# Hybrid attention block on one core: half of the second query column as three rounded products behind the first key half, and lambda's vectors in a buffer of their own

## The chip, the cores and the metric

The kernel runs on one core of a Trainium2 chip. The core has a matmul engine (TensorE, PE in the profile, with PEld for its weight loads), VectorE (DVE), ScalarE (ACT), GpSimd (POOL) and SyncE (SP), which only issues transfers. Each engine works through its own instructions in order; engines wait for each other through semaphores. The metric is the device time of one execution in microseconds (us).

## The reference

A decoder block over 16 meta tokens and 512 positions of width 1024. It normalises the rows, projects them to ten column groups, runs two attention branches, gates and merges them, projects once more and normalises again. What matters here is the first projection and the first attention unit (differential attention, 8 heads, two score maps per head):

```python
h = layer_norm(concat(meta, x), emb_ln_g, emb_ln_b)              # 528 x 1024
lam = exp(sum(lp[0] * lp[1])) - exp(sum(lp[2] * lp[3])) + lam_init
proj = einsum('bld,dn->bln', h, w_in)                            # q_d k_d v_d g_d q_s k_s v_s g_s m_d m_s
s = q k^T / 8 + alibi                                            # two maps per head
a = softmax(s[0]) - lam * softmax(s[1])
y_d = rms_norm(a v, diff_subln_g) * (1 - lam_init)
...
h = layer_norm(DN_ALPHA * h + y, ln_g, ln_b)
```

Everything is float32. Only rows of 512 positions leave the kernel; the meta tokens serve as keys and values.

## The kernel before

The block is laid out with channels on the 128 partitions and positions along the free dimension. hF holds the normalised and scaled input in 8 blocks of channels (k = 0 to 7), each 528 positions wide. A projection of 128 output columns is a sum over the 8 blocks.

**Two kinds of product.** Most products are made of three "rounded" ones: a float32 number a is split into a rounded high part (hTh for the input, wh for a weight) and the rest (hTl, wl), and wh·hTh + wh·hTl + wl·hTh is summed in PSUM. A weight half (4 blocks k) is split by `hi` (ACT makes wh) and `lo` (DVE makes wl) into one of six buffers called w2; four of the eight halves loaded first (raw0) are numbered 0 to 3 for the two query columns, 4 and 5 for the first keys, 6 and 7 for the first values. The two query columns of the first two heads are an exception: `query` multiplies plain float32 operands, one matmul for each k, so it needs no split of hF and can start as soon as a block of hF exists.

**The beginning** is written out by hand in `order`, a string of short steps which are issued in this order to all engines: `S`, `N` statistics and normalisation of a block of 128 positions; `tij` transposes (PE); `aik` scale and shift into hF (ACT; `d` the same on DVE); `xik` the first query column for block i and channel block k (128 positions wide); `yhk` the second query column for half h (256 positions wide); `shk` and `hhk` the high part hTh of half h on ACT and on DVE; `lhk` the low part hTl (DVE); `Hnc`, `Lnc` the weight splits of half 2n+c; `meta`, `hm`, `lm` the meta tokens' part; `lam0`, `lam1`, `lam2` the two sums, the exponentials and the final value of lambda.

**Then** come `q_hi` and `q_lo`, which split the query columns from PSUM (ACT and DVE), and `stage_k` for the first unit: `proj_pos` makes two halves of 264 positions, each 24 matmuls in its own PSUM bank; each finished half is copied out by a chain of six steps that alternate between ACT and DVE (L637 to L642). `stage_v` does the same for values (two more banks). The function `then`, called at time 2.7 of the little clock in `run`, splits the second query column. The scores (`logits`, L764) use two PSUM banks in turn, and each is released by the DVE step at L844, which adds the bias and takes the minimum. The tile scheduler then orders the instructions of each engine; `keep_order` fixes that order as far as the first value stage.

**Memory.** The pool `start` holds what only the beginning needs (inputs, rows, lambda's vectors, sums). It is closed before the pool `att` is opened, which lies in the same memory: the first writer of each `att` tile waits until the last reader of the `start` tiles under it is done. On POOL the first such writers are own_block (L595), the bias ramp (L826 to L829) and the zeros of the key tiles (L607).

Of the kernel before, what the change touches and what calls it, by code (L numbers as in the profile page):

```python
# [9 lines left out]
F32 = mybir.dt.float32  # L10
# [6 lines left out]
P = 128  # L17
D = 1024
KT = D // P
S = 512  # L20
M = 16
# [4 lines left out]
LAM_INIT = 0.8 - 0.6  # L26
# [20 lines left out]
def hybrid_block_kernel(ctx: ExitStack, tc: tile.TileContext, x, meta, emb_g, emb_b, w_in, b_gate,  # L47
                        diff_lambda, subln_g, w_br_d, w_br_s, w_out, ln_g, ln_b, out):
    nc = tc.nc
    v, s, g, pe = nc.vector, nc.scalar, nc.gpsimd, nc.tensor  # L50
# [6 lines left out]
    const = ctx.enter_context(tc.tile_pool(name="const", bufs=1))  # L57
# [3 lines left out]
    gpool = ctx.enter_context(tc.tile_pool(name="g", bufs=6))  # L61
# [3 lines left out]
    pj = ctx.enter_context(tc.tile_pool(name="pj", bufs=3, space=PSUM))  # L65
# [109 lines left out]

    def hi(h):

        assert len(split) == h
        item = items[h]
        assert not second.get(item)  # L180
        raw = raw0[:, h // 2, ts(h % 2, 4)] if item is None else sums.pop(h) if isinstance(item, tuple) else raws[item]
        w2 = wpool.tile([P, 2, 4, P], F32R, tag="w2", name="w2", bufs=6)
        wh, wl = w2[:, 0], w2[:, 1]
        split.append((raw, wh, wl))
        s.copy(wh, raw)  # L185

    def lo(h, eng=v):
# [64 lines left out]
    xts = [sp.tile([P, D], F32, name=f"xt{i}") for i in range(NB)]  # L252
    xns = [sp.tile([P, D], F32, name=f"xn{i}") for i in range(NB)]
    mt = sp.tile([P, D], F32, name="mt")[:M]
    small = sp.tile([P, 512], F32, name="small")
    rows2, lamb = small[:17, :P], small[:, P:P + 256].rearrange("p (a d) -> p a d", a=4)
    for i in range(2):
        for o in (ts(0, 512), ts(1, 512)):
            nc.sync.dma_start(xts[i][:, o], x[0, ts(i, P), o])
# [90 lines left out]
    def q_hi(n):  # L350
        s.activation(A0[n][0], pss[n], AF.Copy, scale=0.125)
        s.activation(A0[n][1][LO], pss[n][HI], AF.Copy, scale=0.125)

    def q_lo(n):
        for c, own, _ in reversed(HEADS):
            v.scalar_tensor_tensor(A0[n][c][HI], pss[n][own], 0.125, A0[n][0][own].bitcast(F32), op0=ALU.mult,
                                   op1=ALU.subtract)
# [79 lines left out]
        tps[1] += banks(SC, SC, TP)  # L437


    lsum = sp.tile([P, 2], F32, name="lsum")  # L440
    lscr = sp.tile([P, 64], F32, name="lscr")
    lexp = sp.tile([P, 2], F32, name="lexp")

    def lam0():
        for c in range(2):
# [6 lines left out]
    def lam2():  # L452
# [5 lines left out]
    steps["t"] = lambda i, j: turn(i, tps[i // 2], range(2 * j, 2 * j + 2))  # L458
    steps["F"] = fill
    steps["H"], steps["L"] = lambda n, c: hi(2 * n + c), lambda n, c: lo(2 * n + c)  # L460
    words = dict(lam0=lam0, lam1=lam1, lam2=lam2, hm=lambda: s.copy(hTh[:, :, :M], hM), lm=low_meta, norm0=norm0, mnorm=mnorm, mturn=mturn, meta=meta, more=more_banks,
                 m0=lambda: stats(4, 0), m1=lambda: stats(4, 1), mr=lambda: rstd(4))

    def order(text):
        for step in text.split():
            if step in words:
                words[step]()
            else:
                steps[step[0]](*map(int, step[1:]))

    order("""S0 norm0 t00 t01 t02 t03 S1 F2 a00 a01 a02 a03 a04 a05 d06 d07 x00 x01 x02 x03 x04 x05 N1 t10 t11 x06 x07 t12 t13
             a10 a11 a12 a13 a14 a15 a16 a17 S2 m0 m1 mr N2 S3 mnorm
             x10 y00 x11 y01 x12 y02 x13 y03 t20 more t21 t22 t23 x14 y04 x15 y05 x16 y06 x17 y07
             a20 a21 a22 a23 a24 a25 a26 a27 H20 H21 x20 x21 x22 x23 N3 t30 t31 t32 t33 x24 x25 x26 x27 mturn
             a30 a31 a32 a33 a34 a35 a36 a37 x30 x31 x32 x33 x34 x35 x36 x37 y10 y11 y12 y13 y14 y15 y16 y17
             h00 h01 h02 h03 l00 l01 l02 l03 L20 L21 meta h04 h05 h06 h07 l04 l05 l06 l07 hm lm lam0
             s10 s11 s12 s13 l10 l11 l12 l13 s14 s15 s16 s17 l14 l15 l16 l17""")
    q_hi(0)
    q_lo(0)
    order("H30 H31 lam1 L30 L31 lam2")  # L480

    def then():
        q_hi(1)
        q_lo(1)

    s.copy(cols[:, 16:33], tm[:, 128:145])
    s.mul(g08, cols[:, 32:33], 1.0 - LAM_INIT)

    start.close()

# [15 lines left out]
    def proj_pos(res, kind, i):  # L506
        n = take(kind, i)
        for c in range(2):
            ps = pj.tile([P, 512], F32, tag="pj", name="ps")
            if n > 4:  # L510
                prep(n + c + state["ahead"])
            for k in range(KT):
                _, wh, wl = split[n + k // 4]
                for m, (a, b) in enumerate(((wh, hTh), (wh, hTl), (wl, hTh))):
                    pe.matmul(ps[:, :H2], a[:, k % 4, :], b[:, k, ts(c, H2)], start=(k == 0 and m == 0),  # L515
                              stop=(k == KT - 1 and m == 2))
                if k < KT - 1:
                    yield 0.33
            res.append(ps)
            if c == 0:  # L520
                yield 0.33
# [52 lines left out]
    def run(proj, steps=()):  # L574

        steps, now = sorted(steps, key=lambda x: x[0]), 0.0
        for part in proj:
            for dt in part:
                now += dt
                while steps and steps[0][0] <= now:  # L580
                    steps.pop(0)[1]()
        for _, step in steps:
            step()


    with tc.tile_pool(name="att", bufs=1) as ap:
# [376 lines left out]
        kept = {x: [dram.tile([P, S], F32, name=f"{x}{j}") for j in range(8)] for x in ("d", "r", "gd", "gs")}  # L963
        for n in range(2):
            units[n]["A"] = A0[n]
        run([stage_k(units[0], *UNITS[0], True)], [(2.7, then)])
        for half in range(2):
            prep(8 + half)
        run([stage_v(units[0], *UNITS[0])])
# [308 lines left out]
```

## Time and profile before

| what | us |
|---|---|
| median of three timed runs | 706.01 (705.26 to 706.11) |
| the profiled execution's own time | 705.09 |
| its span from the first to the last instruction | 703.3 |
| PE busy | 693.3 (99%) |
| DVE busy | 569.5 (81%) |
| ACT busy | 440.5 (63%) |
| POOL busy | 129.8 (18%) |

The granted TensorE clock is 0.998 over the span. A row of the timeline gives the start in us, the busy time of the row in us, engine, line, operation, output and inputs, shape, and how many instructions were merged (x8); a bracket gives the idle time before it and who ended it. A plain float32 matmul stands as two records, so x32 in such a row is 16 matmuls. A matmul's busy time includes its way through the pipeline; how long it keeps the engine is read from the distance between starts. Lines are those of the kernel before; in the changed kernel the same code lies 8 lines further on (L637 becomes L645, L844 becomes L852, L829 becomes L837, L190 becomes L189).

### The profile page before, as it was taken

Reading aid. Unit: us, or ns where it says so; the run is one execution under the profiler, and the core shown is the slowest. Engines: PE = TensorE matmul, PEld = TensorE weight load, DVE = VectorE, ACT = ScalarE, POOL = GpSimd, SP = SyncE. Lnnn points to the kernel's source line nnn. Section 1 sums busy time; section 2 is a strip of 40 time slices with the busy share of each in tenths; the row PEclk is TensorE's granted clock in tenths of the full one; section 3 lists DMA queues with packets and bytes.
Section 4 is the critical chain, followed back from the end, with each engine's and each line's share of the span. In section 5 each row is a group of like instructions: output and inputs, shape, how many; then the busy total and the mean of one; then the engine's idle time right before and its main releaser. Section 6 shows DMA issues by size and latency. Waiting matters only on the chain.

```text
span 703.3 us, 13282 instructions
## 1 busy us (share of the span) xinstructions
PE 693.3 (99%) x4478; PEld 634.1 (90%) x4478; DVE 569.5 (81%) x1225; ACT 440.5 (63%) x1073; POOL 129.8 (18%) x140
## 2 busy tenths in 40 slices
PE   8999999999999999999999999999999999999996
PEld 8999999989899898999989899988888998999885
DVE  6887998878786777899887898977666888688887
ACT  6676767767566687777757687766555456555400
POOL 2243112222222201212121220000012201230011
PEclk9999999999999999999999999999999999999999
DMA  9399557988888796899898977547477749697702
GB/s 292 103 195 182 145 117 178 212 177 184 221 186 182 188 195 183 173 223 206 207 192 219 203 152 194 164 124 242 137 165 142 148 121 245 136 174 194 264 25 116
DMA packets 184215, 124.93 MB, mean 178 GB/s; under 512 B 8994, under 2 KB 168131, under 8 KB 184147
## 3 DMA queue, kind: packets, MB, share of 16 engines
q1 hardware_dynamic: 148050, 102.84, 50.5%
q0 software_dynamic: 35776, 20.19, 23.0%
q10 hardware_dynamic: 320, 1.06, 0.4%
q8 instruction: 35, 0.57, 0.3%
q14 instruction: 34, 0.27, 0.1%
HBM read 93.54 MB, written 9.44 MB: 146 GB/s over the span
## 4 chain that ended last, share of the span: by engine, by line
PE 93%; ACT 2%; SPq 1%; DVE 1%; DMA 1%; issue 0%; DVEq 0%; ACTq 0%
PE q L700 18%; PE ps L501 12%; PE ps L499 12%; PE ps L500 12%; PE q L1083 11%; PE pso L1206 6%; PE ps L515 6%; PE sc L764 6%; PE t L776 4%; PE tv L733 1%; PE av L931 1%; PE av L932 1%; DMA raw<-in_w_in_dram 1%; PE av L925 1%; PE av L933 1%; DMA xt<-in_x_dram 1%
## 5 line engine op out<-in xcount | busy, mean ns | idle before, releaser
L190 DVE TENSOR_TENSOR w<-raw,w 128x512 fp32r<-128x512 f32 x168 | 114.3, 689 | 37.7 <-ACT w L185 36.4
L500 PE MATMUL ps<-hTl,w 128*128 128x512 f32 x368 | 144.9, 394 | 0.0
L499 PE MATMUL ps<-hTh,w 128*128 128x512 f32 x368 | 144.7, 393 | 0.0
L501 PE MATMUL ps<-hTh,w 128*128 128x512 f32 x368 | 144.7, 393 | 0.0
L185 ACT CAST w<-raw 128x512 fp32r<-128x512 f32 x168 | 103.5, 627 | 11.6 <-PE ps L501 5.4
L147 POOL DMA_DIRECT2D rawk<-in_w_in_dram x48 | 66.1, 1630 | 119.5 <-DMA rawk<-in_w_in_dram 66.1
L700 PE MATMUL q<-tS,w 128*128 128x264 f32 x384 | 82.6, 289 | 0.0
L1083 PE MATMUL q<-gh,w 128*128 128x256 f32 x448 | 81.4, 283 | 0.2 <-ACT t L1092 0.2
L501 PEld LDWEIGHTS ps<-hTh,w 128*128 128x128 f32 x368 | 69.2, 188 | 13.5
L500 PEld LDWEIGHTS ps<-hTl,w 128*128 128x128 f32 x368 | 69.2, 188 | 13.1
L499 PEld LDWEIGHTS ps<-hTh,w 128*128 128x128 f32 x368 | 69.2, 188 | 13.0
L1083 PEld LDWEIGHTS q<-gh,w 128*128 128x128 f32 x448 | 70.2, 192 | 0.5 <-ACT t L1092 0.4
L764 PE MATMUL sc<-k,A 128*128 128x264 f32 (+3 forms) x320 | 66.0, 299 | 0.0
L700 PEld LDWEIGHTS q<-tS,w 128*128 128x128 f32 x384 | 63.7, 189 | 0.3
L1083 PE MATMUL q<-gl,w 128*128 128x256 f32 x224 | 63.5, 283 | 0.0
L700 PE MATMUL q<-hTh,w 128*128 128x264 f32 x288 | 60.8, 286 | 0.0
L916 DVE TENSOR_TENSOR_SCAN e<-e,diag 128x528 f32<-128x528 f32 (+1 forms) x64 | 54.2, 850 | 5.6 <-ACT e L910 5.6
L700 PE MATMUL q<-tl,w 128*128 128x264 f32 x192 | 54.9, 286 | 0.0
L764 PEld LDWEIGHTS sc<-k,A 128*128 128x128 f32 x320 | 50.1, 189 | 2.2
L515 PE MATMUL ps<-hTh,w 128*128 128x264 f32 x256 | 51.5, 289 | 0.2 <-ACT k L642 0.2
L700 PEld LDWEIGHTS q<-hTh,w 128*128 128x128 f32 x288 | 47.8, 189 | 1.0
L781 ACT CAST ah<-t 128x384 fp32r<-128x384 f32 (+2 forms) x72 | 34.3, 477 | 21.7 <-PE t L776 21.6
(284 smaller groups left out, 1572.1 us busy)
## 6 DMA issues: line engine op xcount, KB each, us to landing
raw<-in_w_in_dram SPq DMA_DIRECT2D x142, 256.0 KB, 3.4
rawk<-in_w_in_dram POOLq DMA_DIRECT2D x48, 256.0 KB, 5.7
rawk<-in_w_in_dram SPq DMA_DIRECT2D x36, 256.0 KB, 4.1
k<-ks SPq DMA_DIRECT2D x60, 132.0 KB, 3.0
raw<-in_w_out_dram SPq DMA_DIRECT2D x16, 256.0 KB, 4.0
k<-ks SPq DMA_DIRECT2D x60, 66.0 KB, 2.7
A<-low SPq DMA_DIRECT2D x28, 128.0 KB, 3.1
raw<-in_w_br_diff_dram SPq DMA_DIRECT2D x12, 256.0 KB, 3.3
```

The lines of the kernel that those rows point to most:

```text
L147: second[l] = [lambda raw=raw, x=x: g.dma_start(raw, x, accum_op=ALU.add) for x in more]
L185: s.copy(wh, raw)
L190: eng.tensor_tensor(wl, raw, wh.bitcast(F32), op=ALU.subtract)
L499: pe.matmul(ps, wh[:, k % 4, :], hTh[:, k, M:], start=(k == 0), stop=False)
L500: pe.matmul(ps, wh[:, k % 4, :], hTl[:, k, M:], start=False, stop=False)
L501: pe.matmul(ps, wl[:, k % 4, :], hTh[:, k, M:], start=False, stop=(k == KT - 1))
L515: pe.matmul(ps[:, :H2], a[:, k % 4, :], b[:, k, ts(c, H2)], start=(k == 0 and m == 0), stop=(k == KT - 1 and m == 2))
L700: pe.matmul(bank, a[:, k, :], b, start=start and k == 0 and j == 0, stop=k == 3 and j == 2, skip_group_check=not start)
L764: pe.matmul(ps[:, :n], q, K[:, m, k0:k0 + n], start=(m == 0), stop=(m == 1))
L916: v.tensor_tensor_scan(rev, rev, diag[0][:, L - nk:][:, ::-1], 0.0, ALU.mult, ALU.max)
L1083: pe.matmul(bank, a[:, k, :], b[:, n, k, :], start=start and k == 0 and m == 0, stop=k == 3 and m == 2, skip_group_check=not start)
L1206: pe.matmul(ps, MH[k][:, ts(t, P)] if m == "h" else ML[:, k, ts(t, P)], WO[c]["hl".index(w)][:, k, r], start=(n == 0), stop=(n == 3 * KT - 1))
```

## The change

The second half (positions 272 to 527) of the second query column is no longer made by eight plain float32 matmuls (`y10` to `y17`) but by 24 rounded ones in the new function `first_query`, which is issued behind the first key half and uses the split weight halves 2 and 3 (`H10`, `H11`, `L10`, `L11`). The order of the beginning is rewritten with it: four high parts of half 0 go from DVE to ACT (`s00` to `s03`), two low parts (`l00`, `l01`) and the meta tokens' transposes (`mturn`) move ahead, the high parts of half 1 move on ACT ahead of the query split, and the meta tokens' high part goes from ACT to DVE. Lambda's vectors leave the pool `start` for a buffer of the pool g, its sums go to a pool that is never closed, `lam0` moves behind the weight splits of the values, and `lam1` and `lam2` into `then`. The second key half gets the bank of the pool pav instead of one of the three banks of the pool pj.

```diff
     def hi(h):
-        assert len(split) == h
...
-        split.append((raw, wh, wl))
+        split[h:h + 1] = [(raw, wh, wl)]
...
-    small = sp.tile([P, 512], F32, name="small")
-    rows2, lamb = small[:17, :P], small[:, P:P + 256].rearrange("p (a d) -> p a d", a=4)
+    small = sp.tile([P, P], F32, name="small")
+    side = gpool.tile([P, S], F32, tag="sg", name="side")
+    rows2, lamb = small[:17, :P], side[:, :256].rearrange("p (a d) -> p a d", a=4)
...
-    lsum = sp.tile([P, 2], F32, name="lsum")
-    lscr = sp.tile([P, 64], F32, name="lscr")
-    lexp = sp.tile([P, 2], F32, name="lexp")
+    lsum = const.tile([P, 2], F32, name="lsum")
+    lscr = side[:, 256:320]
+    lexp = const.tile([P, 2], F32, name="lexp")
...
-    words = dict(..., hm=lambda: s.copy(hTh[:, :, :M], hM), ...)
+    words = dict(..., hm=lambda: v.tensor_copy(hTh[:, :, :M], hM), ...)
...
     order("""S0 norm0 t00 t01 t02 t03 S1 F2 a00 a01 a02 a03 a04 a05 d06 d07 x00 x01 x02 x03 x04 x05 N1 t10 t11 x06 x07 t12 t13
-             a10 a11 a12 a13 a14 a15 a16 a17 S2 m0 m1 mr N2 S3 mnorm
+             a10 a11 a12 a13 a14 a15 a16 a17 s00 s01 s02 s03 S2 m0 m1 mr N2 S3 mnorm l00 l01
              x10 y00 x11 y01 x12 y02 x13 y03 t20 more t21 t22 t23 x14 y04 x15 y05 x16 y06 x17 y07
-             a20 a21 a22 a23 a24 a25 a26 a27 H20 H21 x20 x21 x22 x23 N3 t30 t31 t32 t33 x24 x25 x26 x27 mturn
-             a30 a31 a32 a33 a34 a35 a36 a37 x30 x31 x32 x33 x34 x35 x36 x37 y10 y11 y12 y13 y14 y15 y16 y17
-             h00 h01 h02 h03 l00 l01 l02 l03 L20 L21 meta h04 h05 h06 h07 l04 l05 l06 l07 hm lm lam0
-             s10 s11 s12 s13 l10 l11 l12 l13 s14 s15 s16 s17 l14 l15 l16 l17""")
+             a20 a21 a22 a23 a24 a25 a26 a27 H20 H21 x20 x21 x22 x23 N3 mturn t30 t31 t32 t33 x24 x25 x26 x27
+             H10 a30 a31 a32 a33 a34 a35 a36 a37 x30 x31 x32 x33 x34 x35 x36 x37 H11 s10 s11 s12 s13 s14 s15 s16 s17
+             L20 L21 meta hm lm l02 l03 h04 h05 h06 h07 l04 l05 l06 l07 L10 L11 l10 l11 l12 l13 l14 l15 l16 l17""")
     q_hi(0)
     q_lo(0)
-    order("H30 H31 lam1 L30 L31 lam2")
+    order("H30 H31 L30 L31 lam0")
+
+    def first_query():
+        for k in range(KT):
+            _, wh, wl = split[2 + k // 4]
+            for m, (a, b) in enumerate(((wh, hTh), (wh, hTl), (wl, hTh))):
+                pe.matmul(pss[1][:, 256:], a[:, k % 4, :], b[:, k, HALF[1]], start=(k == 0 and m == 0),
+                          stop=(k == KT - 1 and m == 2))
 
     def then():
         q_hi(1)
+        order("lam1")
         q_lo(1)
+        order("lam2")
+        s.mul(g08, cols[:, 32:33], 1.0 - LAM_INIT)
 
     s.copy(cols[:, 16:33], tm[:, 128:145])
-    s.mul(g08, cols[:, 32:33], 1.0 - LAM_INIT)
...
     def proj_pos(res, kind, i):
...
-            ps = pj.tile([P, 512], F32, tag="pj", name="ps")
+            ps = (pj if n > 4 or c == 0 else pav).tile([P, 512], F32, tag="pj" if n > 4 or c == 0 else "av", name="ps")
...
-        run([stage_k(units[0], *UNITS[0], True)], [(2.7, then)])
+        run([stage_k(units[0], *UNITS[0], True)], [(2.5, first_query), (2.7, then)])
```

Three places of the built programs show what moves. In their rows the line stands first, then the operation, output and inputs, and the output's shape; "bank" is a PSUM bank of the beginning (the two query columns, and the transposes), "ps" one of a projection.

On PE, the end of the beginning; first before, then in the change. w_312 and w_314 (w_318 and w_320) are the split weights of the first keys, w_350 and w_368 those of the second query column.

```order
L344 MATMUL bank<-ident,xn_105 128x128 x8
L390 MATMUL bank<-hF,raw_87 128x128 x4
L424 MATMUL bank<-ident,mn 128x16 x8
L425 MATMUL bank<-ident,small 128x17
L390 MATMUL bank<-hF,raw_87 128x128 x8
L390 MATMUL bank<-hF,raw_87 128x256 x8
L515 MATMUL ps<-hTh,w_312 128x264
L515 MATMUL ps<-hTl,w_312 128x264
```

```order
L424 MATMUL bank<-ident,mn 128x16 x8
L425 MATMUL bank<-ident,small 128x17
L344 MATMUL bank<-ident,xn_105 128x128 x8
L390 MATMUL bank<-hF,raw_87 128x128 x12
L523 MATMUL ps<-hTh,w_318 128x264
...
L523 MATMUL ps<-hTh,w_320 128x264
L485 MATMUL bank<-hTh,w_350 128x256
L485 MATMUL bank<-hTl,w_350 128x256
```

The eight 256-wide plain matmuls ahead of the keys are gone, the meta transposes stand ahead of the last block's, and the 24 rounded matmuls (L485) follow the first key half.

On DVE, from the last block's normalisation to the first key copy; first before, then in the change. w_412 and w_414 (w_408 and w_410) are the values' weights.

```order
L340 TENSOR_SCALAR xn_105<-xt_101,xmv,xrs 128x512 x2
L396 CAST hTh<-hF 128x256 x4
L401 TENSOR_TENSOR hTl<-hF,hTh 128x256 x4
L190 TENSOR_TENSOR w_312<-raw_87,w_312 128x512
...
L401 TENSOR_TENSOR hTl<-hF,hTh 128x256 x8
L356 SCALAR_TENSOR_TENSOR A_172<-bank,A_171 64x512
L356 SCALAR_TENSOR_TENSOR A_171<-bank,A_171 64x512
L190 TENSOR_TENSOR w_412<-raw_87,w_412 128x512
L190 TENSOR_TENSOR w_414<-raw_87,w_414 128x512
L453 TENSOR_SCALAR nlam<-lexp 128x1
```

```order
L401 TENSOR_TENSOR hTl<-hF,hTh 128x256 x2
L340 TENSOR_SCALAR xn_105<-xt_101,xmv,xrs 128x512 x2
L189 TENSOR_TENSOR w_318<-raw_87,w_318 128x512
...
L396 CAST hTh<-hF 128x256 x4
L401 TENSOR_TENSOR hTl<-hF,hTh 128x256 x4
L189 TENSOR_TENSOR w_350<-raw_87,w_350 128x512
L189 TENSOR_TENSOR w_368<-raw_87,w_368 128x512
L401 TENSOR_TENSOR hTl<-hF,hTh 128x256 x8
L356 SCALAR_TENSOR_TENSOR A_173<-bank,A_172 64x512
L356 SCALAR_TENSOR_TENSOR A_172<-bank,A_172 64x512
```

Two low parts go ahead of the normalisation, four casts leave DVE, two weight splits come in, and lambda's final step is no longer there; it now stands behind the second query's split (`then`).

On PE, from the second value half to the second unit's keys (w_544, in the change w_566); first before, then in the change.

```order
L515 MATMUL ps<-hTh,w_414 128x264
L764 MATMUL sc<-k_442,A_171 128x264 x2
L764 MATMUL sc<-k_443,A_172 128x264 x2
L515 MATMUL ps<-hTh,w_544 128x264
L515 MATMUL ps<-hTl,w_544 128x264
L515 MATMUL ps<-hTh,w_544 128x264 x2
```

```order
L523 MATMUL ps<-hTh,w_410 128x264
L772 MATMUL sc<-k_437,A_172 128x264 x2
L772 MATMUL sc<-k_438,A_173 128x264 x4
L772 MATMUL sc<-k_437,A_172 128x400 x2
L523 MATMUL ps<-hTh,w_566 128x264
L523 MATMUL ps<-hTl,w_566 128x264
L772 MATMUL sc<-k_438,A_173 128x400 x2
L523 MATMUL ps<-hTh,w_566 128x264 x2
```

Where two score tiles stood in a row, five now stand within two matmuls of each other, on the same two banks. From about 370 PE instructions on (of some 4,400) the order of every engine is the same in both programs.

More of the change, by code (lines that the diff above doesn't have):

```diff
@@ L460, in hybrid_block_kernel @@
     steps["H"], steps["L"] = lambda n, c: hi(2 * n + c), lambda n, c: lo(2 * n + c)
-    words = dict(lam0=lam0, lam1=lam1, lam2=lam2, hm=lambda: s.copy(hTh[:, :, :M], hM), lm=low_meta, norm0=norm0, mnorm=mnorm, mturn=mturn, meta=meta, more=more_banks,
+    words = dict(lam0=lam0, lam1=lam1, lam2=lam2, hm=lambda: v.tensor_copy(hTh[:, :, :M], hM), lm=low_meta, norm0=norm0, mnorm=mnorm, mturn=mturn, meta=meta, more=more_banks,
                  m0=lambda: stats(4, 0), m1=lambda: stats(4, 1), mr=lambda: rstd(4))
```

## The prediction

> **What bounds the kernel now.** I read the page's first part, then what PE waited for over the whole span, then the timeline of each engine from 17 to 45 us, where the change lies.
>
> ```profile
> span 703.3 us, 13282 instructions
> PE 693.3 (99%) x4478; PEld 634.1 (90%) x4478; DVE 569.5 (81%) x1225; ACT 440.5 (63%) x1073; POOL 129.8 (18%) x140
> PE warm L309 <- POOL ident masks.py:199: 1.4, 1, 1.4
> PE bank L344 <- DVE xn L340: 1.2, 1, 1.2
> PE ps L515 <- ACT k L642: 0.2, 1, 0.2
> PE q L1083 <- ACT t L1092: 0.2, 1, 0.2
> ```
>
> PE is the bound from the first transposes on: four waits of 0.2 to 1.4 us are all it has (us in total, times, longest). So a microsecond that PE loses or wins in the beginning reaches the end whole; behind about 45 us every engine has the same order in both programs. The question is at what time PE reaches the keys of the second unit.
>
> ```profile
> 18.59 1.04 PE L344 MATMUL bank<-ident,xn 128*128 128x128 f32 x8
> 19.47 1.06 PE L390 MATMUL bank<-hF,raw 128*128 128x128 f32 x8
> 20.45 0.66 PE L424 MATMUL bank<-ident,mn 16*128 16x16 f32 x8
> 21.11 5.51 PE L390 MATMUL bank<-hF,raw 128*128 128x128 f32 x32
> 26.27 0.47 PE L515 MATMUL ps<-hTh,w 128*128 128x264 f32 x1
> 32.26 0.58 PE L764 MATMUL sc<-k,A 128*128 128x264 f32 x2
> 33.05 0.39 PE L515 MATMUL ps<-hTh,w 128*128 128x264 f32 x1 [0.21 <-ACT k L642]
> 38.95 0.65 PE L764 MATMUL sc<-k,A 128*128 128x264 f32 x4
> 39.44 0.29 PE L515 MATMUL ps<-hTh,w 128*128 128x264 f32 x1
> ```
>
> Read by starts: transposes, four first-query matmuls, meta transposes, then (21.11 to 26.27) eight first-query and eight second-query matmuls; 48 key matmuls to 32.26 (0.125 each); one score tile; a pause; 48 value matmuls from 33.05 to 38.95 (0.123 each); two score tiles (0.245 each); the second unit's keys at 39.44. The pause is longer than the 0.21 shown: the score tile is issued by 32.5, so 0.55 us pass. It ends when ACT has emptied the first key bank (L642).
>
> **PE's part of the change.** The eight pairs take 5.16 us, 0.645 a pair. With one third for the 128-wide and two thirds for the 256-wide matmul the latter costs 0.43; from four first-query matmuls in 20.45 - 19.47 = 0.98 it would be 0.40. Removed: 8 x 0.43 = 3.4 us (lower bound 3.2). Added: 24 rounded matmuls of 256 columns at 0.12 (the key matmuls' 0.123 to 0.125 for 264), 2.9 us. PE work: -0.5 us. The meta transposes (0.66) only move ahead of the last block's. So in the change t3 starts at 18.59 + 0.66 = 19.25, takes 0.88 (18.59 to 19.47), then 0.98, then 8 x 0.215 = 1.7, and the first key half starts at 22.85 instead of 26.27. The plain matmuls were cover for DVE's work on hTh and hTl; with them gone PE asks 3.4 us sooner for what DVE and ACT make. So the time has to come from these two.
>
> ```profile
> 17.12 1.00 DVE L340 TENSOR_SCALAR xn<-xt,xmv,xrs 128x512 f32<-128x512 f32 x2 [0.71 <-POOL xrs L300]
> 18.04 0.89 DVE L396 CAST hTh<-hF 128x256 fp32r<-128x256 f32 x4
> 18.85 1.43 DVE L401 TENSOR_TENSOR hTl<-hF,hTh 128x256 fp32r<-128x256 f32 x4
> 20.19 1.28 DVE L190 TENSOR_TENSOR w<-raw,w 128x512 fp32r<-128x512 f32 x2
> 24.68 2.77 DVE L401 TENSOR_TENSOR hTl<-hF,hTh 128x256 fp32r<-128x256 f32 x8
> 27.48 1.41 DVE L356 SCALAR_TENSOR_TENSOR A<-bank,A 64x512 fp32r<-64x512 f32 x2
> 30.13 0.21 DVE L453 TENSOR_SCALAR nlam<-lexp 128x1 f32<-128x1 f32 x1
> 30.90 0.42 DVE L638 TENSOR_TENSOR k<-ps,k 64x264 fp32r<-64x264 f32 x1
> 35.73 0.42 DVE L638 TENSOR_TENSOR k<-ps,k 64x264 fp32r<-64x264 f32 x1
> 36.08 0.41 DVE L844 CUSTOM_DVE_ANT_0 e<-sc,bias 128x264 f32<-128x264 f32 x1
> 30.50 0.37 ACT L637 CAST k<-ps 64x264 fp32r<-64x264 f32 x1 [3.03 <-DVE nlam L453]
> 32.63 0.38 ACT L642 CAST k<-ps 64x264 fp32r<-64x264 f32 x1 [0.50 <-DVE k L641]
> 37.46 0.38 ACT L642 CAST k<-ps 64x264 fp32r<-64x264 f32 x1 [0.50 <-DVE k L641]
> ```
>
> **DVE's part.** DVE has no pause from 17.12 to the first key copy at 30.90: 13.8 us. Taken out: four casts, 18.85 - 18.04 = 0.8; two low parts that move into the 0.71 us idle ahead of 17.12, half of 20.19 - 18.85, 0.7; lambda's last step, 0.25. Put in: two weight splits, 1.2; the meta cast, 0.3 as a link of a dependent chain; about 0.3 more for the wait on the meta transposes (they end at 19.25, DVE comes at 19.25 and takes them up some 0.2 later) and one link more. Sum +0.05: the first key copy on DVE comes at about 30.95, as late as before, although PE is done with that half at 25.9. ACT's 3.03 us of waiting for lambda is no gain, since DVE's turn decides. Lambda's steps themselves are hidden: the sums stay on DVE ahead of the copy, the exponential lies in ACT's pause.
>
> From there on the chain goes as before with two steps between: between the two splits of the second query stands the first minimum (0.43), and lambda's last step (0.2). The second half's DVE copy comes 35.73 - 30.90 = 4.83 + 0.6 later, at 36.4, and ACT's last copy ends 37.46 + 0.38 - 35.73 = 2.1 after that, at 38.5. PE meanwhile: keys, second query, keys and values without a wait (first key half to 25.95, second query to 28.85, keys to 31.75, values with the first score tile to 37.8), then score tiles two and three to 38.3. Tile four needs the last key copy: 38.55, a wait of 0.25. Tiles five and six need their bank free, and the third key product of unit 2 the split of its weights, all behind four minima on DVE (0.43 each, one small step) and a split (0.69): about 0.2 and 0.3 more. That product starts at about 40.35. Before, the same work was done at 39.44 + 2 x 0.12 + 0.245 + 2 x 0.37 = 40.65. So without anything else the change gains 0.3 us, although PE has 0.5 less to do and no pause at 32.5.
>
> **What POOL does to DVE.** The memory released earlier lets POOL start earlier:
>
> ```profile
> 30.54 0.20 POOL L595 MEMSET own_block<- 128x128 f32 x1 [13.45 <-DVE nlam L453]
> 32.95 0.63 POOL L827 TENSOR_SCALAR_AFFINE_SELECT bias<-bias 128x528 f32<-128x528 f32 x1
> 33.67 1.55 POOL L829 TENSOR_SCALAR bias<-bias 128x528 f32<-128x528 f32 x1
> 35.36 1.52 POOL L829 TENSOR_SCALAR bias<-bias 128x528 f32<-128x528 f32 x1
> 77.43 1.25 DVE L678 TENSOR_TENSOR tl<-hF,tS 128x1056 fp32r<-128x1056 f32 x1
> 77.68 2.40 POOL L829 TENSOR_SCALAR bias<-bias 128x528 f32<-128x528 f32 x1 [11.59 <-DVE mn L844]
> 78.60 1.11 DVE L190 TENSOR_TENSOR w<-raw,w 128x512 fp32r<-128x512 f32 x1
> 101.08 2.08 POOL L829 TENSOR_SCALAR bias<-bias 128x528 f32<-128x528 f32 x1
> 101.66 1.14 DVE L879 TENSOR_TENSOR sql<-sq,sqh 128x512 fp32r<-128x512 f32 x1
> 149.07 1.83 POOL L829 TENSOR_SCALAR bias<-bias 128x528 f32<-128x528 f32 x1 [2.10 <-DVE mn L844]
> 149.99 0.69 DVE L190 TENSOR_TENSOR w<-rawk,w 128x512 fp32r<-128x512 f32 x1 [0.48 <-ACT w L185]
> L190 DVE TENSOR_TENSOR w<-raw,w 128x512 fp32r<-128x512 f32 x168 | 114.3, 689 | 37.7 <-ACT w L185 36.4
> ```
>
> POOL waited 13.45 us for lambda's last step. In the change that is no longer under its tiles; the last transposes of the input are (they end about 19.25 + 0.88 + 0.2), so it starts near 20.3, and its three reading operations (L827, L829 twice) come 2.4, 3.1 and 4.8 us later, at 22.7, 23.4 and 25.1. There DVE runs low parts and weight splits back to back, each with two operands in SBUF. Before, they met steps that read PSUM or nothing at all. What such a meeting costs stands at 77 and 101 us: POOL begins while a DVE step with two SBUF operands runs, is drawn out (2.40 and 2.08 instead of 1.5), and the next DVE step takes 1.11 and 1.14 instead of 0.689. So each reading POOL operation costs DVE 0.43 us, once. Three of them: 1.3 us (two, if L827 has no such cost: 0.85; none: 0). DVE's chain has no slack here, so all that follows in it moves. The low parts of half 1 come 1.3 later; PE waits for one of them in `first_query`, about 0.2. The first key copy goes to 32.25, the second to 37.7, ACT's last to 39.8. PE then waits for score tile two (0.6), four (0.8), five and six and the split (0.5); the product that was at 40.65 comes at about 41.65: +1.0 us. With two meetings it is +0.55. I take +0.8, nearer to three, because DVE has no gap in which a meeting could be free.
>
> The Trainium skill, page "SBUF — State Buffer", section "Who interferes with whom", has this as an exclusive lock: a VectorE instruction with two SBUF inputs contends with a GpSimd instruction that reads SBUF, and the later one is fully blocked until the first is done. By that rule taken literally POOL's whole length would be lost; the trace shows less, 0.43 of 1.5 us.
>
> **The sum.** PE's and DVE's own changes -0.3, POOL's three readings +1.1 (1.3 where the chain is the bound, less what falls into PE's slack, and some doubt on the first of them): +0.8 us. The profiled execution took 705.09 (span 703.3, 1.8 around it), so 705.9 for one like it; the three timed runs have their median 0.9 higher, at 706.01, and on that scale I predict 706.8 us. What this measurement can tell from no change is about 0.2%, 1.4 us; so this is "no difference" with a lean to slower.
>
> **The rivals.**
> - *POOL's readings cost nothing.* They may fall behind DVE's steps, or POOL may still be held by another tile until 30 us. For it: the L829 at 149.07 cost DVE nothing (0.69 at 149.99). Against it: DVE was idle for 0.48 us there. Then -0.3: 705.7 us.
> - *DVE and ACT keep up.* If the key copies run ahead of my chain by 1 us, PE has no wait at the score tiles: -0.5 of work and -0.55 of pause, 704.9 us. For it: PE's shift of 3.4 us is real. Against it: the unbroken DVE rows.
> - *Slower: the casts are blocked too.* POOL's memsets (30.54 to 32.95, 2.4 us of writing) now lie over the four casts h04 to h07, which run at 0.2 us for 256 columns, twice as fast as a low part. If each waits for a POOL step, up to 0.8 us more on the same chain: +1.5, 707.5 us. It decides as soon as these four casts take over 1.5 us instead of 0.89. No row shows such a meeting.
> - *POOL holds DVE for its whole length,* 0.63 + 1.55 + 1.52 = 3.7 us: -0.3 + 3.7 = +3.4, 709.4 us. The rows of 1.11 and 1.14 speak against it. This is the skill's rule above.
>
> **Chances.** Forecast 0.48, POOL free 0.22, keeping up 0.12, casts blocked 0.14, whole length 0.04. Faster by over 0.2% (below 704.6) needs nearly all of "keeping up" and a lucky median: 0.07. Slower by over 0.2% (above 707.4): over half of "casts blocked", all of "whole length", a tail of the forecast: 0.17. Within: 0.76. The likeliest case alone is 706.2 to 707.3; the range that leaves out 2 in 10 is 705.0 to 707.7.
>
> **What would show it.** In the changed profile: the first key matmul at about 22.9; own_block near 20.3; L837 twice between 23 and 27 us at over 1.6 us each; two or three DVE steps there that take 1.0 to 1.1 instead of 0.69 or 0.7 to 0.85 instead of 0.41; the first key copy on DVE (L646) at about 32.2; PE waits at L772 that add up to 1 to 2 us between 37 and 41. A key copy near 31.0 and DVE steps of usual length prove me wrong towards 705.7; PE without waits at L772 towards 704.9; casts of twice their length towards 707.5.

## The result, and the profile after

The changed kernel takes 708.80 us (median, 708.13 to 712.89) against 705.83 us (705.09 to 706.37) of the kernel before, run beside it, so the medians are 3.0 us apart. The ratio, which isn't that of the medians, is 1.0054, 95% interval 1.0042 to 1.0065; that would be 3.8 us (3.0 to 4.6). The forecast was 706.8 us, with a range up to 707.7. The profiled execution took 710.16 us, 1.4 more than the median, with a span of 708.4.

The first part of the changed kernel's page:

```profile
span 708.4 us, 13299 instructions
PE 695.1 (98%) x4486; PEld 634.7 (90%) x4486; DVE 572.5 (81%) x1224; ACT 442.3 (62%) x1078; POOL 132.9 (19%) x140
```

What PE waited for in it (us in total, times, longest; the waits shorter than 0.7 and the warm-up are left out):

```profile
PE bank L390 <- DMA raw<-in_w_in_dram: 1.6, 2, 0.9
PE bank L485 <- DVE hTl L401: 1.3, 1, 1.3
PE sc L772 <- DVE mn L852: 0.7, 1, 0.7
```

PE is still the bound, but three waits are new: 1.6 us for the first weights, which nothing in the prediction spoke of, 1.3 us for a low part inside `first_query`, and 0.7 us at the score tiles. The timeline of the changed kernel shows where they come from, PE first, then POOL, then DVE:

```profile
13.34 2.66 PE L390 MATMUL bank<-hF,raw 128*128 128x256 f32 x14 [0.91 <-DMA raw<-in_w_in_dram]
15.84 1.04 PE L344 MATMUL bank<-ident,xn 128*128 128x128 f32 x8
24.65 0.37 PE L523 MATMUL ps<-hTh,w 128*128 128x264 f32 x1
29.43 0.39 PE L485 MATMUL bank<-hTl,w 128*128 128x256 f32 x1 [1.29 <-DVE hTl L401]
71.70 0.60 PE L741 MATMUL tv<-ident,vT 128*128 128x128 f32 x4
17.59 1.31 POOL L299 TENSOR_TENSOR lne<-xmv,epsr 128x1 f32<-128x1 f32 x1 [1.11 <-DVE xmv L327]
22.27 0.20 POOL L603 MEMSET own_block<- 128x128 f32 x1 [2.74 <-ACT hF L384]
23.62 1.23 POOL L615 MEMSET k<- 64x528 f32 x2
24.93 0.76 POOL L835 TENSOR_SCALAR_AFFINE_SELECT bias<-bias 128x528 f32<-128x528 f32 x1
25.78 1.58 POOL L837 TENSOR_SCALAR bias<-bias 128x528 f32<-128x528 f32 x1
28.04 1.97 POOL L837 TENSOR_SCALAR bias<-bias 128x528 f32<-128x528 f32 x1
23.47 1.73 DVE L396 CAST hTh<-hF 128x256 fp32r<-128x256 f32 x4
25.12 2.27 DVE L401 TENSOR_TENSOR hTl<-hF,hTh 128x256 fp32r<-128x256 f32 x4
28.54 3.21 DVE L401 TENSOR_TENSOR hTl<-hF,hTh 128x256 fp32r<-128x256 f32 x8
35.17 0.41 DVE L646 TENSOR_TENSOR k<-ps,k 64x264 fp32r<-64x264 f32 x1
```

Three things are to be seen. The third block's transposes (L344) start at 15.84 instead of 14.21, behind a wait for weights. POOL starts at 22.27 instead of 30.54, and under it DVE's four casts take 1.73 us (before 0.89), four low parts 2.27 (before 1.43) and eight low parts 3.21 (before 2.77): 2.1 us more. And ahead of it all POOL's L299, a step on one column, takes 1.31 us.

What two of the casts lose shows in single rows: POOL's two steps on the keys' zeros (L615), and the second and the third of the four casts.

```profile
23.62 0.61 POOL L615 MEMSET k<- 64x528 f32 x1
23.67 0.71 DVE L396 CAST hTh<-hF 128x256 fp32r<-128x256 f32 x1
24.18 0.68 POOL L615 MEMSET k<- 64x528 f32 x1
24.30 0.70 DVE L396 CAST hTh<-hF 128x256 fp32r<-128x256 f32 x1
```

Each of these two casts starts under one of POOL's steps and ends 0.15 us after it; the first and the fourth take 0.29 and 0.28 us, as casts do that meet nothing.

As mark for PE's place I use the third group of value transposes (L741): 71.70 here. It lies behind the stretch in which the orders differ, so that the same work is done ahead of it in both kernels. Before, the same group, POOL's L299 and its step on the keys' zeros stood so:

```profile
67.82 0.60 PE L733 MATMUL tv<-ident,vT 128*128 128x128 f32 x4
15.82 0.64 POOL L299 TENSOR_TENSOR lne<-xmv,epsr 128x1 f32<-128x1 f32 x1 [1.11 <-DVE xmv L327]
31.86 1.02 POOL L607 MEMSET k<- 64x528 f32 x2
```

### The profile page after: what moved, and what is told of

Same layout as the page of the kernel before. It is cut to its first block, busy times and chain, and to the rows that moved or that the text cites. A ratio compares the mean times of both kernels' runs of the same rounds, so it can differ in the third digit from the quotient of the medians.

```text
span 708.4 us, 13299 instructions
## 1 busy us (share of the span) xinstructions
PE 695.1 (98%) x4486; PEld 634.7 (90%) x4486; DVE 572.5 (81%) x1224; ACT 442.3 (62%) x1078; POOL 132.9 (19%) x140
## 4 chain that ended last, share of the span: by engine, by line
PE 92%; DVE 3%; SPq 2%; ACT 1%; issue 1%; DMA 1%; DVEq 0%; POOL 0%; POOLq 0%; ACTq 0%
PE q L708 17%; PE ps L507 12%; PE ps L508 12%; PE ps L509 12%; PE q L1091 11%; PE pso L1214 6%; PE sc L772 6%; PE ps L523 5%; PE t L784 4%; PE tv L741 1%; PE av L939 1%; DVE hTl L401 1%; PE av L940 1%; DVE w L189 1%; PE av L934 1%
```

## The experiments

Twelve kernels ran. In the table "loads" is the landing time of the 512 KB weight loads, "casts" and "low parts" are the busy times of the four and four steps of DVE that the change's profile showed stretched, "block 3" is the start of the third block's transposes on PE, "key copy" that of DVE's first step on a finished key half, "mark" the start of the third group of value transposes on PE; all these are from one profile each. The ratio is to the kernel before in the same call.

| kernel | loads | block 3 | casts | low parts | key copy | mark | median | ratio, 95% |
|---|---|---|---|---|---|---|---|---|
| before | 6.7 | 14.21 | 0.89 | 1.43 | 30.90 | 67.82 | 705.83 | |
| the change | 7.9 | 15.84 | 1.73 | 2.27 | 35.17 | 71.70 | 708.80 | 1.0054 (1.0042 to 1.0065) |
| after_again | 7.8 | 14.71 | 1.73 | 2.27 | 34.07 | 70.63 | 708.96 | 1.0042 (1.0029 to 1.0056) |
| after_hold | 8.1 | 14.84 | 0.89 | 1.43 | 32.03 | 68.37 | 706.35 | 1.0013 (1.0004 to 1.0022) |
| after_oldlam | 6.6 | 14.25 | 0.89 | 1.43 | 31.79 | 67.78 | 706.12 | 1.0006 (0.9997 to 1.0014) |
| before_lam | 8.6 | 15.72 | 0.92 | 1.41 | 33.45 | 70.30 | 707.18 | 1.0023 (1.0014 to 1.0032) |
| before_shift | 8.3 | 15.17 | 0.89 | 1.43 | 31.99 | 68.85 | 706.32 | 1.0003 (0.9993 to 1.0012) |
| after_align | 7.1 | 14.11 | 1.74 | 2.28 | 33.45 | 70.08 | 708.04 | 1.0032 (1.0020 to 1.0045) |
| hold_align | 7.1 | 14.04 | 0.89 | 1.42 | 31.05 | 67.58 | 706.06 | 1.0001 (0.9992 to 1.0010) |
| hold_align_l0 | 7.2 | 14.40 | 0.89 | 1.43 | 31.52 | 67.92 | 706.14 | 1.0003 (0.9994 to 1.0012) |
| writes_early | 6.8 | 14.04 | 1.82 | 1.42 | 32.47 | 69.04 | 707.67 | 1.0033 (1.0020 to 1.0045) |
| lam_late | 7.2 | 14.52 | 0.89 | 1.42 | 31.04 | (other order) | 708.42 | 1.0042 (1.0028 to 1.0055) |
| old_order_lam_late | 6.9 | 14.35 | 0.89 | 1.42 | 30.17 | (other order) | 705.48 | 0.9997 (0.9989 to 1.0006) |
| lam_gap | 6.8 | 14.28 | 0.89 | 1.42 | 30.42 | 67.40 | 705.47 | 0.9998 (0.9989 to 1.0007) |

From block 3 to the mark PE needs 53.6 us before, 53.5 in the four kernels of the new order whose POOL starts late (after_hold, after_oldlam, hold_align, hold_align_l0), and 55.9 to 56.0 in the three profiles of the new order with POOL early. Of the 5.1 us by which the span of the change's profile is longer, 1.6 stand at block 3 and 2.3 between block 3 and the mark. The other 1.2 come later. Among them are a wait of PE for ACT near 495 us (0.2 us here, none in before, 0.9 in before_shift) and the last store, which lands 2.0 us after its issue in the profiles of before, before_lam, before_shift and lam_late, 2.4 to 2.6 us in the ten others. Where these two come from is open.

### The change once more

> The changed kernel once more, unedited, for a second profile. Theory POOL (the earlier POOL work stretches DVE's casts and low parts): 708.5 to 709.2 us, and this profile shows the same stretched rows (four casts over 1.5 us, four low parts over 2 us). Theory DMA (the change itself makes the first loads land later): PE's waits for raw near 9 and 13 us come again, over 1 us together, and the first key product near 24.6. If these waits were of that one execution, they are under 0.7 us together and the first key product comes at about 23.

The stretched rows came again to the hundredth (1.73, 2.27, 3.21 us), so they belong to the kernel. The wait for raw was 0.2 us this time, at 12.21 us, and the third block's transposes started at 14.71. So 1.1 of the 3.9 us at the mark were of the first profile alone; some delay of the loads stayed.

### POOL held back

```diff
+    hold = const.tile([P, 1], F32, name="hold")
+    g.tensor_copy(hold, split[6][2][:, 0, 0:1].bitcast(F32))
+    behind("hold")
+
     start.close()
...
                 g.iota(bias, ...)
+                behind("hold")
                 g.affine_select(bias, bias, ...)
```

> The changed kernel, but POOL's work after the start waits for the split of weight half 6, so that it begins near 30 us as before the change; nothing moves on PE, DVE, ACT or SP. Theory POOL: the four casts return to about 0.9 us, the low parts to 1.45 (four) and 2.8 (eight), the first key copy on DVE (L646) to about 31, and the time to 705.5 to 706.6. Theory DMA: at most 0.5 us better than the changed kernel for this reason, 708.2 or more; the rest stays as late loads. Theory order (the rounded products and their waits are what costs): 708.3 to 709.

This one step makes POOL wait until DVE has split weight half 6; PE, ACT and SP do the same in the same order. On DVE the tile scheduler made one move that the expectation did not foresee: the first minimum of the scores (L852) stands between the two splits of the second query in the change, and behind the second key copy here, as it did before the change. The timeline of POOL and DVE:

```profile
30.84 0.58 POOL L498 COPY hold<-w 128x1 f32<-128x1 f32 x1 [12.29 <-DVE w L189]
22.49 0.89 DVE L396 CAST hTh<-hF 128x256 fp32r<-128x256 f32 x4
23.30 1.43 DVE L401 TENSOR_TENSOR hTl<-hF,hTh 128x256 fp32r<-128x256 f32 x4
25.85 2.76 DVE L401 TENSOR_TENSOR hTl<-hF,hTh 128x256 fp32r<-128x256 f32 x8
```

All three groups are back at their length of before, and the time falls by 2.6 us between the medians of the same call (708.96 to 706.35), by 2.0 us in the ratio. The theory that the rounded products cost the time is out; the theory POOL stands, with 0.9 us left over. The moved minimum has a part in it: from the first key copy to the second it takes 4.93 us here and 5.40 in the change. The first key copy lies ahead of it and isn't touched. The same move is in after_oldlam, hold_align and hold_align_l0.

### Lambda's tiles as before

```diff
-    side = gpool.tile([P, S], F32, tag="sg", name="side")
+    small = sp.tile([P, 512], F32, name="small")
...
-    lsum = const.tile([P, 2], F32, name="lsum")
+    lsum = sp.tile([P, 2], F32, name="lsum")
...
-    order("H30 H31 L30 L31 lam0")
+    order("H30 H31 lam1 L30 L31 lam2")
...
```

> The changed kernel with lambda's three tiles and its three steps as they were before the change (so POOL waits for lambda's last step again, and the memory of the start comes free later for the loads too); the rounded products and the new order stay. Theory POOL: 705.6 to 706.8 (0.2 us for lambda's last step, which lies ahead of the key copy again). Theory DMA with lambda's load as the cause: 705.6 to 706.8 too, but with PE's waits for raw near 9 and 13 us gone and the casts still long. Theory order: 708.3 to 709.

706.12 us. This undoes one half of the change and keeps the other (the rounded products); nearly the whole loss goes. Unlike with POOL held, the loads land in 6.6 us here and PE doesn't wait for raw.

### Lambda's tiles alone, in the old order

```diff
...
-    rows2, lamb = small[:17, :P], small[:, P:P + 256].rearrange("p (a d) -> p a d", a=4)
+    side = gpool.tile([P, S], F32, tag="sg", name="side")
+    rows2, lamb = small[:17, :P], side[:, :256].rearrange("p (a d) -> p a d", a=4)
...
+    lsum = const.tile([P, 2], F32, name="lsum")
+    lscr = side[:, 256:320]
+    lexp = const.tile([P, 2], F32, name="lexp")
```

> The kernel before with lambda's buffers alone moved as in the change (its steps stay where they were): POOL may begin some 10 us earlier under the old order. Theory POOL: DVE's four casts and its low parts are stretched here too, by 1.3 to 2.8 us together, the first key copy comes at 32 to 33.5 instead of 30.9, and the time is 707.1 to 708.6. Theory DMA (buffer of its own makes the loads late): PE waits for raw near 9 and 13 us, 706.8 to 707.8, casts of 0.9 us. Theory order: 705.6 to 706.1, no difference to before.

1.7 us slower than before without a single rounded product. In the profile the loss has two parts, and the theory DMA names one of them rightly: the loads land late and PE waits 1.2 us for raw, so that block 3 starts 1.5 us later than before; from there to the mark PE needs 1.0 us more, which is POOL's part. Its timeline (POOL's three reading steps, then DVE from the second group of casts on) shows the price of one meeting most clearly, since each step meets another one:

```profile
24.43 1.05 POOL L608 MEMSET k<- 64x528 f32 x2
25.55 0.79 POOL L828 TENSOR_SCALAR_AFFINE_SELECT bias<-bias 128x528 f32<-128x528 f32 x1
26.44 1.58 POOL L830 TENSOR_SCALAR bias<-bias 128x528 f32<-128x528 f32 x1
28.24 1.70 POOL L830 TENSOR_SCALAR bias<-bias 128x528 f32<-128x528 f32 x1
23.60 0.92 DVE L397 CAST hTh<-hF 128x256 fp32r<-128x256 f32 x4
24.45 1.41 DVE L402 TENSOR_TENSOR hTl<-hF,hTh 128x256 fp32r<-128x256 f32 x4
25.78 0.70 DVE L435 TENSOR_TENSOR hTl<-hM,hTh 128x128 fp32r<-128x128 f32 x1
26.66 0.52 DVE L447 CUSTOM_DVE_ANT_0 side<-side 128x64 f32<-128x64 f32 x1
27.11 3.20 DVE L402 TENSOR_TENSOR hTl<-hF,hTh 128x256 fp32r<-128x256 f32 x8
```

L435 takes 0.70 instead of 0.28, the second sum of lambda 0.52 instead of 0.22, the eight low parts 3.20 instead of 2.77: 0.42, 0.30 and 0.43 us for the three reading steps of POOL, one each. The four low parts that lie over the keys' zeros (L608, which only writes) keep their 1.41 us. The casts keep theirs too: here they are all but done when the zeros begin. They do lie over four smaller writes (L598, 32x32), and there it is POOL that takes longer, 0.80 us instead of 0.58.

### The addresses

The landing times fall into two groups, and what the slow ones share is an address. In the built programs of before and of after_oldlam the buffers of the start's loads begin at multiples of 256 bytes. Lambda's two small tiles, put into the constants, push everything behind them up by 64 bytes (96 with the tile for the hold). Two kernels move that alone:

```diff
     ident = const.tile([P, P], F32, name="ident")
+    const.tile([P, 16], F32, name="pad64")
```

> The kernel before with one unused 64-byte tile in the constants, which moves every buffer behind them by 64 bytes, as lambda's two small tiles do in the change; nothing else. Theory address (the start's loads land later when their destinations do not begin at a multiple of 256 bytes): the 512 KB loads land 7.7 to 8.6 us after their issue instead of 6.7, PE waits 0.2 to 1.2 us for raw at 11.6 to 13.3 us, and the time is 705.9 to 706.6. Theory chance: no wait for raw, 705.2 to 705.8 as before.

```diff
-    lsum = const.tile([P, 2], F32, name="lsum")
+    lsum = const.tile([P, 56], F32, name="lsum")[:, :2]
```

> The changed kernel with 192 bytes more in the constants, so that the buffers behind them begin at multiples of 256 bytes again; POOL still starts early. Theory address: no wait for raw, the third block's transposes at about 14.2 us, 707.9 to 708.5. Theory chance: 708.6 to 709.1.

The large weight loads among the transfers of before_shift up to 20 us (size, then median us from issue to landing):

```profile
raw<-in_w_in_dram SPq DMA_DIRECT2D x3, 512.0 KB, 8.3
```

and PE's wait in its timeline:

```profile
12.67 2.66 PE L391 MATMUL bank<-hF,raw 128*128 128x256 f32 x14 [0.78 <-DMA raw<-in_w_in_dram]
```

The same loads in after_align:

```profile
raw<-in_w_in_dram SPq DMA_DIRECT2D x3, 512.0 KB, 7.1
```

and in its timeline the third block's transposes, ahead of which no wait for raw is left:

```profile
14.11 1.04 PE L344 MATMUL bank<-ident,xn 128*128 128x128 f32 x8
```

In the table all five programs with shifted buffers have 7.8 to 8.6 us, all nine with multiples of 256 have 6.6 to 7.2. So the landing is settled, and with it PE's start: block 3 comes at 14.0 to 14.5 us in these nine and at 14.7 to 15.8 in the five. (The loads of 256 KB show it less clearly: 5.1 to 5.6 us against 5.5 to 6.7.) What it is worth at the end is less sure: 0.0003 in the ratio in the old order, 0.0010 from after_again to after_align, 0.0012 from after_hold to hold_align, that is 0.2 to 0.85 us, and each of the three alone could be chance by its interval. The Trainium skill, page "DMA: Bandwidth & Descriptors", section "How a descriptor splits into AXI transactions", says that a transaction must start at a multiple of 256 bytes and that, where a descriptor doesn't, the bytes ahead of its start are fetched unused and still cost beats (of 32 bytes). It says so of reads; what moves in these runs is the address that is written, and that such a splitting is the reason was not shown.

### Both mended, and the two low parts

> POOL held until the split of weight half 6 and the addresses restored, both together. Theory POOL plus address: 705.6 to 706.0 and no wait of PE for raw. Theory POOL alone: 706.2 to 706.5 as with POOL held alone. If the order of the change costs something by itself, what stays above 705.5 here is its size.

```diff
-             ... S2 m0 m1 mr N2 S3 mnorm l00 l01
+             ... S2 m0 m1 mr N2 S3 mnorm
...
-             ... N3 mturn t30 ...
+             ... N3 l00 l01 mturn t30 ...
```

> The one before with the two low parts l00 and l01 behind the last block's norm, where they take their 0.74 us of DVE, instead of in the wait for POOL's rstd. Theory rstd (in the wait they hold POOL's L299 up by 0.67 us, so that the gap was not free): L299 at 0.64 instead of 1.31 us, the last norm 0.67 earlier, the first key copy within 0.15 us of the one before, the time within 0.2 us of it. Theory free gap (as predicted): 0.5 to 0.7 us slower than the one before.

With POOL held and the addresses restored the change stands where the kernel before stands: 1.0001 (0.9992 to 1.0010). What is left of the new order is +0.1 us, with 0.6 to either side; from block 3 to the mark it is 53.54 us against 53.61. Rows of hold_align: POOL's rstd, DVE's two low parts and the last norm, PE's first key matmul, the first key copy.

```profile
15.63 1.31 POOL L299 TENSOR_TENSOR lne<-xmv,epsr 128x1 f32<-128x1 f32 x1 [1.11 <-DVE xmv L327]
16.14 0.74 DVE L401 TENSOR_TENSOR hTl<-hF,hTh 128x256 fp32r<-128x256 f32 x2
17.60 1.00 DVE L340 TENSOR_SCALAR xn<-xt,xmv,xrs 128x512 f32<-128x512 f32 x2 [0.72 <-POOL xrs L300]
22.85 0.37 PE L527 MATMUL ps<-hTh,w 128*128 128x264 f32 x1
31.05 0.41 DVE L650 TENSOR_TENSOR k<-ps,k 64x264 fp32r<-64x264 f32 x1
```

and of hold_align_l0, the rstd and the norm:

```profile
16.10 0.64 POOL L299 TENSOR_TENSOR lne<-xmv,epsr 128x1 f32<-128x1 f32 x1 [1.11 <-DVE xmv L327]
17.40 1.00 DVE L340 TENSOR_SCALAR xn<-xt,xmv,xrs 128x512 f32<-128x512 f32 x2 [0.71 <-POOL xrs L300]
```

DVE waits 0.72 us for the rstd with the two low parts ahead of it and 0.71 without them: the gap isn't filled, it moves back, because POOL's L299 takes 1.31 us instead of 0.64 while DVE reads two SBUF operands. From rstd to norm the way is 0.67 us shorter without them, and the two low parts then cost their 0.74 behind it. The times agree (706.06 and 706.14). The first key copy came 0.47 later rather than within 0.15, since this profile runs 0.36 later from its first transposes on; the difference that the order makes is 0.1.

### POOL's writes and reads apart

```diff
                 g.iota(bias, pattern=[[-1, L]], base=400, ...)
+                behind("hold")
+                g.tensor_copy(hold, split[6][2][:, 0, 0:1].bitcast(F32))
+                behind("hold")
                 g.affine_select(bias, bias, ...)
...
```

> The changed kernel with its addresses restored and POOL held only behind its writing steps: own_block, the two memsets of the keys' tiles and the iota run early as in the change, the three reading steps (L835, L837 twice) wait for the split of weight half 6. Theory two kinds (POOL's writes stretch DVE's casts, POOL's reads its low parts): the four casts stay at 1.5 to 1.8 us, the low parts return to 1.43 (four) and 2.77 (eight), the first key copy comes at about 31.9, the time is 706.5 to 707.1. Theory reads alone: casts of 0.9 us and 705.9 to 706.2. Theory writes alone: casts long and no part of the loss left out, 707.5 or more.

The timeline of POOL, and the two groups of DVE in question:

```profile
21.37 1.16 POOL L615 MEMSET k<- 64x528 f32 x2
22.61 0.57 POOL L836 IOTA bias<- 128x528 f32 x1
30.98 0.58 POOL L838 COPY hold<-w 128x1 f32<-128x1 f32 x1 [7.80 <-DVE w L189]
21.70 1.82 DVE L396 CAST hTh<-hF 128x256 fp32r<-128x256 f32 x4
23.45 1.42 DVE L401 TENSOR_TENSOR hTl<-hF,hTh 128x256 fp32r<-128x256 f32 x4
```

With nothing but writes on POOL the casts still take 1.82 us, and the low parts are free of it. So there are two kinds of meeting, and both are in the change. The Trainium skill, page "SBUF — State Buffer", section "Who interferes with whom", says the same of the kinds: a copy or cast that VectorE runs in a two-port mode contends with any GpSimd instruction, an instruction with two SBUF inputs only with one that reads. The casts' 0.22 us for 256 columns, against 0.36 for a low part of the same size, fit a faster mode. The order of DVE is that of the change here, so after_align and this kernel differ in POOL's reading steps alone: without them PE needs 55.0 us from block 3 to the mark instead of 56.0.

The first key copy came later than expected (32.47 instead of about 31.9), and the time was higher, 707.67 instead of 706.5 to 707.1. It lies where the theory writes alone put it, and the ratio is that of after_align (1.0033 and 1.0032), so that the times by themselves don't show what the reads cost; the rows do. Against hold_align the mark is 1.5 us later. Up to the second key copy DVE has lost 1.7 us against it: 0.9 at the casts, 0.3 where the reading steps, now at 31.5 us, meet one sum of lambda (0.53 instead of 0.22 us), and 0.5 by the first minimum, which stands ahead of the second key copy here and behind it in hold_align.

### Lambda out of DVE's chain

> POOL held and addresses restored, and lambda's three steps moved behind the first values, out of DVE's chain ahead of the key copies (0.5 us of sums ahead of the first, 0.2 us more ahead of the second). Theory chain (DVE's chain to the key copies sets PE): first key copy at about 30.6, second at 35.4 to 35.6, 0.3 to 0.6 us faster than without this step, 705.4 to 705.8. Theory PE (with POOL out of the way PE is the bound already): no difference, 705.9 to 706.2.

> The same treatment (POOL held, addresses, lambda's steps late) for the old order without the rounded products. If the new order is worth the 0.3 us of the prediction, this is 0.3 us slower than the one before; if it is worth nothing, both are the same within 0.3 us; theory chain expects 705.3 to 705.7 here, since lambda's steps leave the chain in the old order as well.

Both put the three steps of lambda behind the first values (`run([stage_v(...)], [(1.0 + m, f) for m, f in enumerate((lam0, lam1, lam2))])`). Neither tells what it should. The tile scheduler answered with another order: PE's order in lam_late differs from that of hold_align through most of the kernel, more of the first unit's scores went ahead of the transposes of its values, and later PE waited 1.4 us at a score tile for keys that a transfer brings. From the last norm to the first key copy the chain did become 0.43 us shorter (18.02 to 31.04, where hold_align has 17.60 to 31.05), and the kernel was 0.0041 of the ratio, some 2.9 us, slower than hold_align. The old order with the same treatment is at 0.9997 and can't be compared with it. The next one moves less:

```diff
     def then():
         q_hi(1)
-        order("lam1")
+        order("lam0 lam1")
+        side_signs[0]()
         q_lo(1)
...
```

> POOL held and addresses restored, and two pieces of DVE work moved from ahead of the first key copy into the 1.67 us in which DVE waits for ACT between the key halves: lambda's sums (0.5 us) and the two steps that make sides (0.35 us). Some twenty instructions between 38 and 50 us change places, the rest keeps its order. Theory chain (DVE's chain to the key copies still sets PE): first key copy 0.8 us earlier than with POOL held and addresses restored alone (30.2 to 30.5 instead of 31.05), second 0.7 earlier, PE's waits at the score tiles under 0.3 us, 705.2 to 705.7, which is 0.3 to 0.7 us below the kernel before. Theory PE (nothing left to win there): 705.9 to 706.2.

Here (`side_signs[0]()` runs the two steps that make the tile sides) the order of PE changes by some 30 lines. In its timeline the first key copy comes 0.63 us earlier than in hold_align:

```profile
30.42 0.42 DVE L656 TENSOR_TENSOR k<-ps,k 64x264 fp32r<-64x264 f32 x1
```

and apart from the warm-up the list of PE's waits has one line:

```profile
PE q L1102 <- ACT t L1111: 0.2, 1, 0.2
```

705.47 us is 0.9998 of the kernel before (0.9989 to 1.0007): as good as before, and no better that could be told. On PE the theory chain is borne out: from block 3 to the mark it is 53.12 us, 0.42 less than in hold_align and 0.49 less than before. A gain of that size can't be told in the times.

## Why the prediction was wrong

The sign of the lean was right, and the cause in part: POOL's early start, of which the sum counted the reads and put the writes at nothing. The size was not: +0.8 us were forecast, +3.0 measured. In the words of its steps:

- **PE's part** was right. With POOL and the addresses out of the way the first key half starts at 22.85 us, the forecast's own number, and the first key copy on DVE at 31.05 (forecast: about 30.95). That the second number is so near is partly luck: the last norm comes 0.65 us later after block 3 than before (17.60 - 14.04 against 17.12 - 14.21), and the way from it to the copy is 0.38 shorter than forecast (13.45 instead of 13.83). Two slips are in the working and change nothing: 24 matmuls of 0.125 behind 22.85 end at 25.85, not 25.95, and a cast is 1.7 times as fast as a low part by the starts, not twice.
- **"Without anything else the change gains 0.3 us"** was measured as +0.1 (0.6 to either side). It is not refuted by that, but on PE only 0.07 us of it are there (53.54 instead of 53.61 from block 3 to the mark). One of its terms is: "two low parts that move into the 0.71 us idle ahead of 17.12, 0.7". That gap was POOL's rstd, and the low parts held the rstd up by 0.67. I took a wait for an empty place without asking whether what goes in slows down what is waited for. The term was lost, and others in the sum (the waits on the meta transposes and the links, put in at 0.3) were smaller than I thought.
- **"Each reading POOL operation costs DVE 0.43 us, once. Three of them: 1.3 us"** was right: 0.84 for L835 and the first L837, 0.44 for the second, 1.28 in all, and the three single meetings in the old order 0.42, 0.30 and 0.43. POOL's small reading copies (L678, 128x32) lie between them in the change and cost DVE nothing that shows; they take 0.74 and 0.49 us themselves instead of 0.20.
- **"The casts are blocked too"**, kept as a rival with 0.14, came true at its upper end: 0.84 us (1.73 instead of 0.89), two casts at 0.42 each. This is the step that failed first: the sum counted POOL's writes with 0. The row that mattered stood in the prediction, the casts' higher speed, and with it the condition, "over 1.5 us instead of 0.89"; I counted it unlikely because no row of before showed such a meeting. A meeting that can't be seen because the cover has never been off is not a meeting that costs nothing. With this term the prediction's own sum is 707.5, by its own price for the rival.
- **PE's wait in `first_query`**, "about 0.2", was 1.29, in after_align too: the low parts of half 1 start 1.95 us later there than in hold_align (26.81 against 24.86; 0.2 of it is that profile's later norm) instead of 1.3, and PE comes to them about as early as forecast. Held back, this wait is gone from the list.
- **The addresses** were in no step and no rival: 0.2 to 0.85 us by the ratios, 0.5 to 1.6 at block 3 in the five profiles (14.71 to 15.84 instead of 14.21). I read of "a pool that is never closed" for lambda's sums what it frees, not what it pushes. The landing of the loads was not among the signs to look for either.
- **POOL holds DVE for its whole length** (+3.4, 0.04) was as far off as thought, though its time, 709.4, is near the measured one: 0.42 to 0.44 us are lost at steps of 0.76 to 1.97 us. The Trainium skill's sentence that the other one is fully blocked for the whole instruction, which the page writes of VectorE's two-port modes, is not borne out for steps with two SBUF operands. The casts agree with it: both that lose time end 0.15 us after POOL's step.

By the medians of runs of one call each, POOL's early start is worth 2.6 us (after_again to after_hold) or 2.0 us (after_align to hold_align), and 2.4 on PE from block 3 to the mark both times; in it is the one minimum that DVE's order moved. The addresses are worth 0.2 to 0.85, the rest 0.1: 2.3 to 3.5 us, around the 3.0 measured. On PE most of the 2.4 us stand in two waits, 1.3 in `first_query` and 0.7 at a score tile.

## What to carry to other kernels

When a change frees memory earlier, look for who was waiting for it: the work that starts sooner may run into the engine that sets the end, and being held back was a service. A short idle stretch ahead of a wait is free only for work that doesn't slow down what is being waited for. And a few bytes in a pool that lies in front of everything move every buffer behind it, so compare the addresses of the transfers before and after.

## What the runs showed of the chip

- A POOL step that only writes (zeros of 64x528, an iota) stretches DVE's 256-column casts from 0.89 to 1.82 us for four, and leaves steps with two SBUF operands at 1.42 for four. A cast that starts under one ends 0.15 us after it.
- A POOL step of 128x528 that reads costs DVE 0.30 to 0.44 us at a step with two SBUF operands, whether it is 0.76 or 1.97 us long.
- It goes the other way too: POOL's step on a single column (L299) takes 1.31 us behind DVE's low parts and 0.64 without them.
- Loads of 512 KB land in 6.6 to 7.2 us where the buffers behind the constants begin at multiples of 256 bytes, and in 7.8 to 8.6 where they begin 64 or 96 bytes further on.
